# Hybrid decoder trunk on one core: both groups of heads through the attention together, and the norm's broadcast two units later

## The chip, the cores and the metric

The kernel runs on one core of a Trainium2 chip. The metric is the device time of one execution in microseconds. Before the change it was 2619.73 us, the median of three runs (2618.04 to 2623.62). The core has five engines that work side by side from queues of their own: TensorE (PE in the profile; its weight loads are PEld), VectorE (DVE), ScalarE (ACT), GpSimd (POOL) and SyncE (SP), which here issues most DMAs.

## What is computed

Two layers of a decoder trunk run over 576 tokens: 512 of a prompt and 8 x 8 of samples, which share all weights. Each layer is a half-step SwiGLU, a mixer with three branches (causal convolution, gMLP, attention), and another half-step SwiGLU. The change lies in the mixer, in its attention and in the layer norm of its gMLP branch:

```python
def sink_attention(q, k, v, mask, sinks):            # 8 q heads, 2 kv heads, head_dim 64
    s = jnp.einsum('...qkgd,...skd->...kgqs', q, k).astype(jnp.float32) * (HEAD_DIM ** -0.5)
    s = jnp.where(mask, s, NEG_INF)
    sk = sinks.astype(jnp.float32).reshape(N_KV_HEADS, Q_PER_KV, 1)
    m = jnp.maximum(jnp.max(s, axis=-1), sk)
    p = jnp.exp(s - m[..., None])
    denom = jnp.sum(p, axis=-1) + jnp.exp(sk - m)
    p = (p / denom[..., None]).astype(v.dtype)
    return jnp.einsum('...kgqs,...skd->...qkgd', p, v)
...
    g_in = jax.nn.gelu(g_in)
    u = g_in[..., :D_GMLP]
    vg = layer_norm(g_in[..., D_GMLP:], ln_gmlp_g, ln_gmlp_b)
    sg = jnp.einsum('gts,bcsgd->bctgd', w_s, vc) + b_spatial[:, :n].T[None, None, :, :, None]
    y_b = (u * sg.reshape(B, L, D_GMLP)) @ w_gmlp_out
```

The prompt's attention is banded: each chunk of 128 queries sees its own 128 keys and the 128 before. The samples see a cache of 128 keys each and the new tokens.

## The kernel before

Everything lies with features on the partitions and the 576 tokens along the free axis. The projections are exact fp32 products made of three fp32r passes (`mm3`, lines 319 to 329): high x high, high x low, low x high, each on two halves of 288 tokens. One weight tile of four K-tiles gives 24 such matmuls; this is called a unit. After each unit `ftile_parts` calls `steps()` (line 340), which moves every generator in `chains` on by one `yield`. So a side computation is written as a generator, and `wait(n)` in it means: n units of projections before what follows.

Two generators run beside the projections of the mixer. `attention()` (line 765) is one, `sgu()` (line 1008) the other. They issue their matmuls through `cpe`, which gives them a high priority and puts them behind the latest projection matmul; their VectorE and ScalarE work goes through `ave` and `ase` at a lower priority than that of the projections (`ve`, `se`), and the convolution's taps go through `lve` at the lowest. A planner then fixes the order of each engine's queue from these priorities and from its own estimate of when inputs are there; on the chip each queue runs in that order. In this helper all such instructions have line 86 or 88 in the profile, so the reader goes by the names of tiles.

In the attention, both groups of heads lie on partitions: q and k of kv head 0 on rows 0 to 63, those of kv head 1 on rows 64 to 127 (`q4` holds four query heads of each group, `kk` the keys). The values are transposed into `vT`, where a group takes 64 columns. After the rotation of q and k, `sample_scores` and `sample_values` do the samples, and then `scores(c, kv)` and `values` do the prompt, chunk by chunk and, within a chunk, first kv head 0 and then 1. `scores` issues four matmuls of 64 rows into two PSUM tiles of the tag `n` (two buffers in all), adds the mask (VectorE) and calls `soft`, the softmax with the sinks on VectorE and ScalarE. `values` transposes the probabilities, copies them to `ptp` and multiplies them by `vT`: 64 columns of output for the group, which ScalarE copies into `q4`. The list `ready` holds the generators of `values` that are under way; from the scores of a (chunk, group) to its transposes pass five units, and from these to its values two. An iteration is three units, so the eight take 24.

`layer_norm` (line 719) gets its waits as a tuple: W_G = (4, 4, 3, 3) for the gMLP branch. The third is handed to `rstd_steps` (line 387), whose matmuls against `ones` sum the squares, whose Newton steps on VectorE (`newton`, tiles nv, nt, no) make the reciprocal root, and whose matmuls against `idr` broadcast it, split in a high part (ScalarE, line 368) and a low part (VectorE, line 369) in the tile `oh`. The third number is the units between the Newton steps and that broadcast. Behind it follow the normalised rows (tile gv) and `spatial(j)`, four times. `drain(sgu_)` (line 1059) and `drain(att)` (line 1074) run out what is left of either generator.

The rotation of q and k, which comes before the sample scores, swaps halves by DMAs on SP's queue (tile rt), multiplies on GpSimd and VectorE and ends in a copy of the samples' q (tile qs).

Of the kernel before, what the change touches and what calls it, by code (L numbers as in the profile page):

```python
# [12 lines left out]
AF = mybir.ActivationFunctionType  # L13
ALU = mybir.AluOpType
PSUM = bass.MemoryType.PSUM

P = 128
# [19 lines left out]


W_V, W_S, W_N, W_T, W_R, W_B = 2, (2, 1, 1, 1, 1), 3, 2, 6, 1
W_M, W_A = 2, 1  # L40
W_G, W_C = (4, 4, 3, 3), (2, 3, 2)
CHUNKS = ((0, 6), (6, 12), (12, 17), (17, KF))

N_PLAIN = 3
# [15 lines left out]
V_SP = V_CB + 22  # L60
# [35 lines left out]
def trunk(ctx: ExitStack, tc: tile.TileContext, a):  # L96
# [7 lines left out]
    cpe = _At(tc, nc.tensor, HI, mark)  # L104
    ave, ase, age, asy = (_At(tc, e, LOW // 2) for e in (nc.vector, nc.scalar, nc.gpsimd, nc.sync))
# [4 lines left out]
    sp = ctx.enter_context(tc.tile_pool(name="sp", bufs=1))  # L110
# [12 lines left out]
    def big(tag, name, dt=F32, n=1024):  # L123
        return sp.tile([P, n], dt, tag=tag, name=name, bufs=2)
# [8 lines left out]
    def mtile(tag="m"):  # L133
        return zp.tile([P, 512], F32, tag=tag, name=tag)
# [16 lines left out]
    ident = idr.bitcast(F32)  # L151
# [3 lines left out]
    def vcol(l, c, n=1):  # L155
        return vec[:, l, c:c + n]
# [62 lines left out]
    raws, ready = {}, {}  # L219
# [114 lines left out]
    def drain(g):  # L334
        for _ in g:
            pass
        if g in chains:
            chains.remove(g)
# [376 lines left out]
    def wait(n):  # L715
        for _ in range(n):
            yield
# [28 lines left out]
    def mixer(l, xd, nxt):  # L746
# [10 lines left out]
        kk = slot("k", "kk")  # L757
# [7 lines left out]
        def attention():  # L765
# [55 lines left out]
            def soft(s4, sink, view, w, tag):  # L821

                m = tp.tile([P, 4], F32, tag=tag + "m", name="m")
                ave.tensor_reduce(out=m, in_=s4, axis=mybir.AxisListType.X, op=ALU.max)
                ave.tensor_tensor(out=view(m), in0=view(m), in1=sink, op=ALU.max)
                ave.tensor_scalar(out=m, in0=m, scalar1=-1.0, scalar2=None, op0=ALU.mult)
                e = tp.tile([P, 4], F32, tag=tag + "e", name="e")
                ave.tensor_tensor(out=view(e), in0=view(m), in1=sink, op=ALU.add)
                ase.activation(out=e, in_=e, func=AF.Exp)
                d = tp.tile([P, 4], F32, tag=tag + "d", name="d")  # L830
                for j in range(4):
                    ase.activation(out=s4[:, j, :], in_=s4[:, j, :], func=AF.Exp, bias=m[:, j:j + 1], accum_out=d[:, j:j + 1])
                ave.tensor_tensor(out=d, in0=d, in1=e, op=ALU.add)
                ave.reciprocal(out=d, in_=d)
                for j in range(4):
                    ase.activation(out=s4[:, j, :], in_=s4[:, j, :], func=AF.Copy, scale=d[:, j:j + 1])
# [7 lines left out]
            s = big("sp", "ss")[:, 0:768]  # L844
            s4 = s.rearrange("p (k n) -> p k n", k=4)

            def sample_scores():
                for kv in range(2):
                    zz = mtile("n")
                    r = slice(64 * kv, 64 * kv + 64)  # L850
                    for g in range(2):
                        for b in range(4):
                            cpe.matmul(out=zz[32 * b:32 * b + 32, 192 * g:192 * g + P],
                                       lhsT=qs[r, 4 * g + b].rearrange("p j t -> p (j t)"),
                                       rhs=ck[r, P * (4 * g + b):P * (4 * g + b + 1)], start=True, stop=True)
                        cpe.matmul(out=zz[:, 192 * g + P:192 * (g + 1)],
                                   lhsT=qs[r, 4 * g:4 * g + 4].rearrange("p b j t -> p (b j t)"),
                                   rhs=kk[r, TP:T], start=True, stop=True)
                    ave.scalar_tensor_tensor(out=s[:, 384 * kv:384 * (kv + 1)], in0=zz[:, 0:384], scalar=0.125,
                                             in1=con[:, C_MS:C_MS + 384], op0=ALU.mult, op1=ALU.add)  # L860
                sk = vcol(l, V_SS, 2).rearrange("p (k o) -> p k o", o=1).to_broadcast([P, 2, 2])
                soft(s4, sk, lambda t: t.rearrange("p (k g) -> p k g", k=2), 192, "x")

            def sample_values():
                pt = big("pt", "pts")
                zt = mtile("n")
                for i in range(4):
                    cpe.transpose(zt[:, P * i:P * (i + 1)], s4[:, i, 0:P], ident)
                ase.activation(out=pt[:, 0:512], in_=zt, func=AF.Copy)
                zt = mtile("n")  # L870
                for i in range(4):
                    cpe.transpose(zt[0:TS, P * i:P * (i + 1)], s4[:, i, P:192], ident)
                ase.activation(out=pt[0:TS, 512:1024], in_=zt[0:TS, :], func=AF.Copy)
                yield
                zo = mtile("n")
                for kv in range(2):
                    r = slice(64 * kv, 64 * kv + 64)
                    for g in range(2):
                        i = 2 * kv + g
                        cpe.matmul(out=zo[r, P * g:P * (g + 1)], lhsT=vT[0:TS, 4, r], rhs=pt[0:TS, 512 + P * i:512 + P * (i + 1)],  # L880
                                   start=True, stop=False, skip_group_check=True)
                        for b in range(4):
                            bb = 4 * g + b
                            cpe.matmul(out=zo[r, 32 * bb:32 * bb + 32], lhsT=cv[:, P * bb + 64 * kv:P * bb + 64 * kv + 64],
                                       rhs=pt[:, P * i + 32 * b:P * i + 32 * b + 32], start=False, stop=True, skip_group_check=True)
                ave.tensor_copy(out=q4[:, :, TP:T].rearrange("p j (b t) -> p b j t", b=NB),
                                in_=zo[:, 0:256].rearrange("p (b j t) -> p b j t", b=NB, j=4))


            def scores(c, kv):  # L890
                o0 = P if c == 0 else 0
                w = 256 - o0
                k0 = max(c - 1, 0) * P
                r = slice(64 * kv, 64 * kv + 64)
                s4 = big("sp", "sp").rearrange("p (j n) -> p j n", j=4)[:, :, 0:w]
                msk = con[:, C_MP + o0:C_MP + 256].rearrange("p (o n) -> p o n", o=1).to_broadcast([P, 2, w])
                for j in (0, 2):
                    z = mtile("n").rearrange("p (i n) -> p i n", i=2)
                    for i in range(2):
                        cpe.matmul(out=z[:, i, 0:w], lhsT=q4[r, j + i, c * P:(c + 1) * P], rhs=kk[r, k0:k0 + w], start=True, stop=True)  # L900
                    ave.scalar_tensor_tensor(out=s4[:, j:j + 2, :], in0=z[:, :, 0:w], scalar=0.125, in1=msk, op0=ALU.mult, op1=ALU.add)
                soft(s4, vcol(l, V_SP + 4 * kv, 4), lambda t: t, w, "p")
                return values(c, kv, s4, w // P, k0, r)

            def values(c, kv, s4, nk, k0, r):
                pt = big("pt", "ptp")
                for b in range(nk):
                    zt = mtile("n")
                    for j in range(4):
                        cpe.transpose(zt[:, j * P:(j + 1) * P], s4[:, j, b * P:(b + 1) * P], ident)  # L910
                    ase.activation(out=pt[:, 512 * b:512 * (b + 1)], in_=zt, func=AF.Copy)
                yield
                zo = mtile("n")
                for b in range(nk):
                    cpe.matmul(out=zo[r, :], lhsT=vT[:, k0 // P + b, r], rhs=pt[:, 512 * b:512 * (b + 1)],
                               start=(b == 0), stop=(b == nk - 1))
                ase.activation(out=q4[r, :, c * P:(c + 1) * P], in_=zo[r, :].rearrange("p (j n) -> p j n", j=4), func=AF.Copy)


            sample_scores()  # L920
            yield
            ready = [sample_values()]
            for c in range(4):
                for kv in range(2):
                    ready.append(scores(c, kv))
                    yield from wait(W_A)
                    if len(ready) > 2:
                        drain(ready.pop(0))
                    yield
                    next(ready[-2])  # L930
                    yield from wait(W_B)
            drain(ready.pop(0))
            yield
            next(ready[0])
            yield from wait(W_B)
            drain(ready[0])

        att = attention()
        next(att)
# [330 lines left out]
```

## Time and profile before

| | |
|---|---|
| median of three runs | 2619.73 us |
| the profiled execution | 2623.66 us |
| its span, first to last instruction | 2621.9 us |
| TensorE busy | 2584.4 us (99%) |
| VectorE busy | 1909.9 us (73%) |
| ScalarE busy | 1273.5 us (49%) |
| mean granted TensorE clock | 0.995 |

The busy time of TensorE is the union of its matmuls' spans, whose ends are modelled; starts are measured. So what a block of matmuls costs the stream is best read from the start of its first to the start of the next matmul that is not of the block. A form like 64*128 64x256 means 64 rows and 128 columns of the array, and 64 partitions x 256 elements that stream through it. Every fp32 matmul leaves two records, each fp32r matmul one.

### The profile page before, as it was taken

The numbers are of one execution on the slowest core, as the hardware profiler recorded it, in microseconds if no ns is written. First come the engines' busy times: TensorE is split into PE (matmuls) and PEld (weight loads), VectorE is DVE, ScalarE is ACT, GpSimd is POOL, SyncE is SP. The second block draws the span as 40 slices with busy tenths as digits, with TensorE's granted clock in tenths as the row PEclk, the third lists the DMA queues.
The fourth block names the chain that finished last, engine by engine and source line by source line (L and its number), as shares of the span: only waits on it lengthen the run. The fifth ranks groups of instructions, "written<-read, shape, count | busy, mean of one in ns | idle before, by whom it ended". The sixth has DMA issues, their size and how long they took to land.

```text
span 2621.9 us, 49387 instructions
## 1 busy us (share of the span) xinstructions
PE 2584.4 (99%) x18996; PEld 2519.7 (96%) x18996; DVE 1909.9 (73%) x3488; ACT 1273.5 (49%) x2415; POOL 286.9 (11%) x317
## 2 busy tenths in 40 slices
PE   8999999999999999999999999999999999999999
PEld 8999999988899999999999999998989999999999
DVE  8676665688897786766885766747988977756665
ACT  6455453335424564554674554532453245644543
POOL 0111010010010021111110111101100100111110
PEclk9999999999999999999999999999999999999999
DMA  6565454231222464655564655533212234655553
GB/s 178 129 147 130 123 121 129 84 88 58 67 83 81 131 151 124 147 124 131 132 136 119 149 125 132 141 103 85 78 57 73 85 104 123 142 126 137 126 135 95
DMA packets 193920, 303.30 MB, mean 116 GB/s; under 512 B 39434, under 2 KB 56714, under 8 KB 193684
## 3 DMA queue, kind: packets, MB, share of 16 engines
q1 hardware_dynamic: 156820, 233.28, 29.5%
q0 software_dynamic: 36720, 66.86, 15.2%
q8 instruction: 149, 2.44, 0.4%
q14 instruction: 87, 0.71, 0.1%
q10 hardware_dynamic: 144, 0.00, 0.0%
HBM read 221.43 MB, written 8.84 MB: 88 GB/s over the span
## 4 chain that ended last, share of the span: by engine, by line
PE 91%; DVE 3%; DMA 3%; issue 1%; ACT 1%; SPq 0%; POOL 0%; DVEq 0%; POOLq 0%; ACTq 0%
PE z L322 18%; PE z L325 17%; PE z L328 17%; PE z L569 14%; PE n L569 9%; PE m L569 9%; PE n L86 4%; PE m L86 2%; DMA wc<-w_gu 2%; DMA w<-wc 1%; DVE w L88 1%; ACT w L88 1%; DVE u L88 0%; DVE sums L88 0%; DVE x L88 0%
## 5 line engine op out<-in xcount | busy, mean ns | idle before, releaser
L88 ACT ACTIVATE w<-wr 128x512 fp32r<-128x512 f32 (+1 forms) x533 | 324.0, 622 | 657.9 <-PE z L328 526.2
L569 PE MATMUL z<-xh,w 128*128 128x288 f32 x2040 | 443.4, 299 | 5.5 <-DVE z L88 3.7
L88 ACT ACTIVATE w<-wc 128x512 fp32r<-128x512 f32 (+2 forms) x509 | 271.5, 565 | 243.3 <-PE z L328 89.1
L88 DVE TENSOR_TENSOR w<-sums,w 128x512 fp32r<-128x512 f32 x340 | 234.1, 689 | 198.5 <-ACT w L88 194.7
L569 PEld LDWEIGHTS z<-xh,w 128*128 128x128 f32 x2040 | 337.5, 188 | 11.8 <-DVE z L88 5.8
L322 PE MATMUL z<-xh,w 128*128 128x288 f32 x1520 | 337.4, 303 | 8.0 <-ACT w L88 6.6
L88 DVE TENSOR_TENSOR w<-wr,w 128x512 fp32r<-128x512 f32 (+2 forms) x373 | 254.3, 682 | 122.0 <-ACT w L88 121.5
L325 PE MATMUL z<-xl,w 128*128 128x288 f32 x1520 | 328.0, 297 | 0.0
L328 PE MATMUL z<-xh,w 128*128 128x288 f32 x1520 | 327.7, 296 | 0.0
L322 PE MATMUL z<-ah,w 128*128 128x288 f32 x1408 | 303.6, 296 | 0.4
L325 PE MATMUL z<-al,w 128*128 128x288 f32 x1408 | 302.1, 296 | 0.6 <-DVE al L88 0.5
L328 PE MATMUL z<-ah,w 128*128 128x288 f32 x1408 | 301.3, 296 | 0.0
L569 PE MATMUL z<-xl,w 128*128 128x288 f32 x1020 | 300.5, 295 | 0.0
L88 ACT ACTIVATE w<-sums 128x512 fp32r<-128x512 f32 x340 | 212.1, 624 | 176.3 <-PE z L569 90.4
L322 PEld LDWEIGHTS z<-xh,w 128*128 128x128 f32 x1520 | 245.6, 191 | 22.1 <-issue 11.7
L325 PEld LDWEIGHTS z<-xl,w 128*128 128x128 f32 x1520 | 248.2, 191 | 0.7 <-issue 0.7
L328 PEld LDWEIGHTS z<-xh,w 128*128 128x128 f32 x1520 | 246.7, 190 | 0.5 <-issue 0.3
L88 DVE SCALAR_TENSOR_TENSOR c<-cb,vec,c 128x512 f32<-128x512 f32 x480 | 244.5, 556 | 0.2
L322 PEld LDWEIGHTS z<-ah,w 128*128 128x128 f32 x1408 | 226.7, 189 | 2.6 <-DVE x L88 2.3
L325 PEld LDWEIGHTS z<-al,w 128*128 128x128 f32 x1408 | 226.6, 189 | 1.8 <-DVE al L88 1.8
L328 PEld LDWEIGHTS z<-ah,w 128*128 128x128 f32 x1408 | 226.6, 189 | 0.0
L88 POOL DMA_DIRECT2D w<-wc x175 | 150.5, 860 | 616.6 <-ACT w L88 221.3
(255 smaller groups left out, 4854.5 us busy)
## 6 DMA issues: line engine op xcount, KB each, us to landing
wc<-w_gu SPq DMA_DIRECT2D x212, 256.0 KB, 2.9
wr<-w_in SPq DMA_DIRECT2D x184, 256.0 KB, 2.8
w<-wc POOLq DMA_DIRECT2D x175, 256.0 KB, 3.7
wr<-w_gu SPq DMA_DIRECT2D x140, 256.0 KB, 2.8
wr<-w_dn SPq DMA_DIRECT2D x92, 256.0 KB, 2.8
w<-wr POOLq DMA_DIRECT2D x80, 256.0 KB, 4.1
wc<-w_dn SPq DMA_DIRECT2D x36, 256.0 KB, 3.0
wr<-w_out SPq DMA_DIRECT2D x32, 256.0 KB, 3.2
```

Of the source, the lines that this page charges most:

```text
L86: r = f(*args, **kw)
L88: r = f(*args, **kw)
L322: pe.matmul(out=z[c], lhsT=wh, rhs=rh[:, s], start=first, stop=False)
L325: pe.matmul(out=z[c], lhsT=wh, rhs=rl[:, s], start=False, stop=False)
L328: e = pe.matmul(out=z[c], lhsT=wl, rhs=rh[:, s], start=False, stop=last)
L569: e = pe.matmul(out=out, lhsT=w[:, k, :], rhs=r, start=first and k == 0 and i == 0, stop=k == n - 1 and i == 2, skip_group_check=True)
```

## The change

The order of work changes in three places.

In the samples' part, the score matmuls of the two groups are issued in turns, first all those against the cache, then those against the new keys, into two PSUM tiles at once. The value matmuls are issued in turns as well.

In the prompt's part, `scores(c)` and `values(c, ...)` handle both groups of a chunk. The score matmuls of the groups alternate, so that neighbours use rows 0 to 63 and rows 64 to 127 and write different PSUM tiles; the value matmuls alternate between the two halves of the columns of one PSUM tile, and one copy over 128 partitions takes the place of two over 64. The list `ready` is gone: W_A goes from 1 to 4, so four units pass between the scores of a chunk and its transposes, and the values of a chunk come right ahead of the transposes of the next. A chunk takes five units, the whole prompt 20.

In W_G the third number goes from 3 to 5.

```diff
-W_M, W_A = 2, 1
-W_G, W_C = (4, 4, 3, 3), (2, 3, 2)
+W_M, W_A = 2, 4
+W_G, W_C = (4, 4, 5, 3), (2, 3, 2)
...
             def sample_scores():
-                for kv in range(2):
-                    zz = mtile("n")
-                    r = slice(64 * kv, 64 * kv + 64)
-                    for g in range(2):
-                        for b in range(4):
-                            cpe.matmul(out=zz[32 * b:32 * b + 32, 192 * g:192 * g + P],
+                zz = [mtile("n") for kv in range(2)]
+                for g in range(2):
+                    for b in range(4):
+                        for kv, r in enumerate(KV):
+                            cpe.matmul(out=zz[kv][32 * b:32 * b + 32, 192 * g:192 * g + P],
                                        lhsT=qs[r, 4 * g + b].rearrange("p j t -> p (j t)"),
                                        rhs=ck[r, P * (4 * g + b):P * (4 * g + b + 1)], start=True, stop=True)
...
-            def scores(c, kv):
+            def scores(c):
...
-                s4 = big("sp", "sp").rearrange("p (j n) -> p j n", j=4)[:, :, 0:w]
+                s4 = [big("sp", "sp").rearrange("p (j n) -> p j n", j=4)[:, :, 0:w] for kv in range(2)]
...
                 for j in (0, 2):
-                    z = mtile("n").rearrange("p (i n) -> p i n", i=2)
+                    z = [mtile("n").rearrange("p (i n) -> p i n", i=2) for kv in range(2)]
                     for i in range(2):
-                        cpe.matmul(out=z[:, i, 0:w], lhsT=q4[r, j + i, c * P:(c + 1) * P], rhs=kk[r, k0:k0 + w], start=True, stop=True)
-                    ave.scalar_tensor_tensor(out=s4[:, j:j + 2, :], in0=z[:, :, 0:w], scalar=0.125, in1=msk, op0=ALU.mult, op1=ALU.add)
-                soft(s4, vcol(l, V_SP + 4 * kv, 4), lambda t: t, w, "p")
-                return values(c, kv, s4, w // P, k0, r)
+                        for kv, r in enumerate(KV):
+                            cpe.matmul(out=z[kv][:, i, 0:w], lhsT=q4[r, j + i, c * P:(c + 1) * P], rhs=kk[r, k0:k0 + w],
+                                       start=True, stop=True)
+                    for kv in range(2):
+                        ave.scalar_tensor_tensor(out=s4[kv][:, j:j + 2, :], in0=z[kv][:, :, 0:w], scalar=0.125, in1=msk,
+                                                 op0=ALU.mult, op1=ALU.add)
+                for kv in range(2):
+                    soft(s4[kv], vcol(l, V_SP + 4 * kv, 4), lambda t: t, w, "p")
+                return values(c, s4, w // P, k0)
...
                 for b in range(nk):
-                    cpe.matmul(out=zo[r, :], lhsT=vT[:, k0 // P + b, r], rhs=pt[:, 512 * b:512 * (b + 1)],
-                               start=(b == 0), stop=(b == nk - 1))
-                ase.activation(out=q4[r, :, c * P:(c + 1) * P], in_=zo[r, :].rearrange("p (j n) -> p j n", j=4), func=AF.Copy)
+                    for kv, r in enumerate(KV):
+                        cpe.matmul(out=zo[r, :], lhsT=vT[:, k0 // P + b, r], rhs=pt[kv][:, 512 * b:512 * (b + 1)],
+                                   start=(b == 0), stop=(b == nk - 1), skip_group_check=True)
+                ase.activation(out=q4[:, :, c * P:(c + 1) * P], in_=zo.rearrange("p (j n) -> p j n", j=4), func=AF.Copy)
...
             sample_scores()
-            yield
-            ready = [sample_values()]
+            yield from wait(W_A)
+            last = sample_values()
+            next(last)
+            yield from wait(W_B)
             for c in range(4):
-                for kv in range(2):
-                    ready.append(scores(c, kv))
-                    yield from wait(W_A)
-                    if len(ready) > 2:
-                        drain(ready.pop(0))
-                    yield
-                    next(ready[-2])
-                    yield from wait(W_B)
-            drain(ready.pop(0))
-            yield
-            next(ready[0])
-            yield from wait(W_B)
-            drain(ready[0])
+                g = scores(c)
+                yield from wait(W_A)
+                drain(last)
+                last = g
+                next(last)
+                yield from wait(W_B)
+            drain(last)
```

## Rows read from the trace of the kernel before

**Rows 1.** The page: busy time by engine (part 1), the chain (part 4).
```profile
PE 2584.4 (99%) x18996; PEld 2519.7 (96%) x18996; DVE 1909.9 (73%) x3488; ACT 1273.5 (49%) x2415; POOL 286.9 (11%) x317
...
PE 91%; DVE 3%; DMA 3%; issue 1%; ACT 1%; SPq 0%; POOL 0%; DVEq 0%; POOLq 0%; ACTq 0%
```

**Rows 2.** TensorE by line and shape: count | busy us, mean ns | idle before.
```profile
L86 PE MATMUL n<-ptp,vT 128*64 128x512 f32 x56 | 27.5, 607 | 0.0
L86 PE MATMUL n<-kk,q 64*128 64x256 f32 x96 | 24.4, 391 | 0.0
...
L86 PE MATMUL n<-kk,q 64*128 64x128 f32 x32 | 4.6, 285 | 0.0
```

**Rows 3.** Timeline of TensorE, waits: start us, us, operation xcount [idle before <-releaser].
```profile
339.58 2.41 PE L569 MATMUL n<-f,w 128*128 128x288 f32 x12 [1.74 <-DVE u L88]
...
535.65 0.82 PE L86 MATMUL m<-idr,oh 128*128 128x128 f32 x2 [3.32 <-ACT oh L368]
...
1829.99 0.55 PE L86 MATMUL m<-idr,oh 128*128 128x128 f32 x2 [2.53 <-ACT oh L368]
...
1831.91 1.80 PE L86 MATMUL m<-idr,oh 128*128 128x128 f32 x8 [0.77 <-DVE oh L369]
...
1868.91 1.11 PE L86 MATMUL n<-idr,ss 128*128 128x128 f32 x6 [0.34 <-ACT ss L88]
```

**Rows 4.** Timeline of TensorE: a score block and the split one, each with its follower.
```profile
596.60 1.99 PE L86 MATMUL n<-kk,q 64*128 64x256 f32 x8
598.52 0.53 PE L322 MATMUL z<-xh,w 128*128 128x288 f32 x2
...
657.45 1.13 PE L86 MATMUL n<-kk,q 64*128 64x256 f32 x4
658.51 0.53 PE L322 MATMUL z<-xh,w 128*128 128x288 f32 x2
```

**Rows 5.** Timeline of TensorE: a values block and its follower.
```profile
648.16 1.93 PE L86 MATMUL n<-ptp,vT 128*64 128x512 f32 x4
650.03 0.53 PE L322 MATMUL z<-xh,w 128*128 128x288 f32 x2
```

**Rows 6.** Timeline of TensorE: the start of the sample scores.
```profile
558.30 0.42 PE L86 MATMUL n<-ck,qs 64*32 64x128 f32 x8
558.66 0.43 PE L86 MATMUL n<-kk,qs 64*128 64x64 f32 x2
559.02 0.42 PE L86 MATMUL n<-ck,qs 64*32 64x128 f32 x8
```

**Rows 7.** Timeline of TensorE: the sample values, the start of two sets.
```profile
584.83 0.43 PE L86 MATMUL n<-pts,vT 64*64 64x128 f32 x2
...
585.77 0.43 PE L86 MATMUL n<-pts,vT 64*64 64x128 f32 x2
```

**Rows 8.** Windows: length, busy us (xcount) by engine, granted clock, DMA share, GB/s.
```profile
535.60:545.40 9.80, 9.67 (x37) 8.96 (x38) 7.50 (x13) 3.40 (x7) 2.27 (x4) 0.50 0.30 87
1830.00:1839.10 9.10, 8.33 (x36) 7.80 (x37) 7.10 (x12) 2.99 (x6) 2.56 (x3) 0.62 0.32 94
340.00:345.00 5.00, 5.00 (x28) 5.00 (x28) 5.00 (x11) 1.60 (x3) 0.18 (x1) 0.66 0.76 168
```

**Rows 9.** Timeline of VectorE: the low part of the factor; the samples' q.
```profile
537.36 0.15 DVE L369 TENSOR_TENSOR oh<-no,oh 128x5 fp32r<-128x5 f32 x1
...
555.77 0.28 DVE L88 COPY qs<-q 128x256 f32<-128x256 f32 x1
```

**Rows 10.** Windows again, PE, PEld, DVE, ACT, POOL in this order.
```profile
533.30:555.80 22.50, 20.07 (x116) 19.36 (x117) 20.18 (x30) 8.74 (x16) 9.24 (x8) 0.77 0.36 86
558.30:600.00 41.70, 41.66 (x336) 37.90 (x336) 39.75 (x97) 20.20 (x60) 4.87 (x6) 1.00 0.24 72
```

**Rows 11.** Timelines of VectorE and ScalarE: a softmax's first and last steps.
```profile
629.80 1.29 DVE L88 SCALAR_TENSOR_TENSOR sp<-n,con 128x512 f32<-128x512 f32 x2
...
637.12 1.70 ACT L88 ACTIVATE sp<-sp,d 128x256 f32<-128x256 f32 x4
```

## What I expect of the change

> **What bounds the kernel now.** I read the page first: TensorE is busy for 99% of the span and the chain that ended last lies on it for 91% [rows 1]. So a microsecond taken out of its stream counts, as long as nobody else becomes late. The stretch that the change touches is the mixer of each layer. Its time splits into the full-width projection matmuls (two of 0.132 us each per merged entry of the timeline) and the attention's small fp32 blocks that are pushed in between. The groups by line show the two large kinds: 96 records of scores and 56 of values [rows 2]; every fp32 matmul leaves two records. The reader should see in the timeline what one such block costs the stream, and that TensorE never idles among them. The one place in this stage where it does idle is the normalisation of the gMLP branch, at 535 us and again at 1830 us [rows 3].
>
> **Scores of the prompt.** A block of 8 records holds TensorE from 596.60 to 598.52, 1.92 us; a block of 4 holds it from 657.45 to 658.51, 1.06 us [rows 4]. So a record costs 0.215 us and entering and leaving the half-height form about 0.20 us a block. Per layer and for blocks 1 to 3 there are six blocks of 8. After, each chunk has two blocks (heads 0 and 1, then 2 and 3), because the four score tiles share two PSUM buffers and the second pair waits for VectorE; each again has 8 records, but 4 of each group of heads, in rows 0 to 63 and 64 to 127. If the two halves of the array run side by side, such a block takes the time of 4 records: 6 x 1.92 = 11.5 us becomes 6 x 1.06 = 6.4, and 5.2 us go (one of the six is already split, which adds 0.2). If they don't, nothing is saved. Chunk 0 has narrower blocks: 4.6 us for the four in both layers [rows 2], 1.15 each; by the same halving 0.9 us a layer.
>
> **Values of the prompt.** Four records take from 648.16 to 650.03, 1.87 us [rows 5], two about 1.0. Both groups now fill the two column halves of one block: three blocks of 1.87 and one of 1.0 fall away a layer, 6.6 us. Merging also halves the evacuations into q4 on ScalarE, which cost nothing either way, since ScalarE is busy for 49% [rows 1].
>
> **Sample part.** The four sets of scores follow each other every 0.72 us (558.30 to 559.02) [rows 6]; issued in pairs, half of 2.87 us goes, 1.4. The four sets of values take 0.94 us each (584.83 to 585.77) [rows 7]; half of 3.76 is 1.9.
>
> **Do packed matmuls overlap in fp32?** For column groups the trace says yes: eight records of the cache scores, four column groups, take 0.42 us and hold the next one off by 0.36, the same as two records alone (0.43 and 0.36) [rows 6]. For row groups no row of before shows it; the bounds are nothing and one half, and I take one half, by the nearest row, the column groups. Sum for a layer 5.2 + 0.9 + 6.6 + 1.4 + 1.9 = 16.0 us, 32 us for both. The Trainium skill (TensorE: Matmul & The Clock Gate, Part 3) gives 3.07x for four row tiles and 2.38x for three column tiles, not 4 and 3; an estimate from its 77%, 1.54x for two, would make the 32 us about 22. The row of four column groups shows no such loss.
>
> **The norm's broadcast.** The program reaches it at 532.33 and idles 3.32 us until ScalarE's half of the factor is there; in layer 1 it idles 2.53 and 0.77 us [rows 3]. The idle time also costs the clock: the granted clock is 0.50 over the next 9.8 us and 0.62 over 9.1 us in layer 1 [rows 8], so 4.9 and 3.5 us more. Together 3.3 + 4.9 = 8.2 and 3.3 + 3.5 = 6.8, 15.0 us. Two units are 48 projection matmuls, 6.3 us, so TensorE would arrive at 538.6 and 1833.8; the later half of the factor ends at 537.5 [rows 9] and was in use at 1831.91 [rows 3]. So this stall goes whole.
>
> **What is late next.** The sample scores need the copy of q, which ends at 556.05, only 2.25 us before they start at 558.30 [rows 6, 9]. That slack existed because TensorE had lost 8.2 us. Behind it stand the rotations of q on VectorE, with their DMAs on SP's queue and the multiply on GpSimd. From 533.3 to 555.8 VectorE is busy for 20.2 of 22.5 us [rows 10], so with all its idle time gone and the two vt operations (0.87 us) moved behind, the copy comes 3.2 us earlier. TensorE would then wait 8.2 - 2.25 - 3.2 = 2.8 us in layer 0; for layer 1, with the same slack, 1.3. The bounds are 0 (the convolution's taps, the lowest priority, fall behind the copy) and these; I take 4.1, because VectorE is the busier of the two there. A wait of 1.74 us at 339.58 was followed by a clock of 0.66 over 5 us [rows 3, 8], 1.7 us lost; I add it once. The norm's part is 15.0 - 4.1 - 1.7 = 9.2 us.
>
> **The other moved waits.** Scores to transposes were five units for one group; now they are four units for two. One group's softmax takes from 629.80 to 638.82 [rows 11], 9.0 us between other work, and two overlap on VectorE and ScalarE; four units are 12.7 us plus the small blocks inside, about 16. That is tight. The one place where a softmax was just late idled TensorE 0.34 us [rows 3]. For eight chunks I take 0.3 us each, 2.4, with bounds 0 and 0.8 each; behind a waiting transpose stand all projection matmuls. The gMLP steps after the broadcast also come two units later, which leaves the last of them (15 small matmuls) to be issued together where the generator is drained, without units between them and their transposes. At worst they wait for one copy and one subtraction, some 1.5 us a layer; I take nothing, since the product that uses them comes three projections later and the score block that is split in two shows that projections are put between blocks that wait [rows 4].
>
> **Sum.** 32.0 + 9.2 - 2.4 = 38.8 us. The profiled execution took 2623.66 us (span 2621.9 and 1.8 around it), 3.9 above the median of the runs shown; the gain has nothing to do with that difference, so 2623.66 - 38.8 = 2584.9 for it, and 2619.73 - 38.8 = 2581 against the median.
>
> **The rivals.**
> - Row halves don't overlap, column halves do. Speaks for it: no row shows two row groups at once. Lost: 5.2 + 0.9 and about 0.9 of the sample scores, 7.0 a layer: 2595 us.
> - Both overlap, but each pass gets slower while a second stream reads its operand. A pair of score passes then takes between 0.215 us (no loss) and 0.43 (no gain); at 0.28, three tenths of the way, 16.0 a layer shrinks by 4.8: 2591 us. Against it: the eight-record row [rows 6]. This is what the 77% of the Trainium skill (same page and part) would do here.
> - The change does not do what it says: no overlap at all. Left are the fewer entries of merged blocks (about 2 us a layer) and the norm: 2609 us.
> - The stall moves whole to the sample scores: idle as computed, and the clock falls as long as it did before, 4.9 + 3.5 instead of 1.7: 2588 us.
> - VectorE becomes the bound. From 558.3 to 600 it is busy 39.75 of 41.7 us [rows 10], while I take about 7 us of TensorE's time out of that stretch; if 5 of these come back in each layer, 2591 us.
> - Slower: the two softmaxes don't fit in four units and TensorE waits at the transposes of all eight chunks, long enough to lose the clock as in layer 1's stall, 6.8 us each: 54 in place of the 2.4, 2633 us. It decides from about 5.2 us a chunk (41.2 / 8). For it: 16 us against a chain of 9 that is run twice; against it: the projections that are put in between.
>
> **How the numbers follow.** Chances: forecast 0.50 (its own range 2567 to 2592), row halves 0.11, slower passes 0.08, no overlap 0.05, moved stall 0.14, VectorE 0.04, two late softmaxes 0.08. The shortest time is full overlap, no new wait and no softmax wait: 32 + 15, 2572 us; with 0.2 us a block on either side of the fixed costs 2567. The range goes up to the rival of the row halves with some of the waits' upper bound, 2600. Left out are no overlap, late softmaxes and a little. A measurement of this kernel can tell 0.2%, 5.2 us. All cases but the last lie further below; of its 0.08, 0.02 fall within (waits of 36 to 46 us in all). So faster 0.92, same 0.02, slower 0.06.
>
> **What would show it.** Right: score blocks of 8 records that take 1.06 us and values blocks of 8 records that take 1.9; starts of the two row groups within a few hundredths of a microsecond; no idle time before the broadcast and the clock at 1.00 after it. Wrong: score blocks of 1.9 us, idle time before the first sample scores above 3 us or before the transposes above 1 us, or a granted clock below 1.00 between 545 and 700 us.

## The result and the profile after

The changed kernel takes 2605.51 us, the median of four runs (2603.23 to 2608.89), against 2620.32 for the kernel before (2618.04 to 2623.62), run beside it. The ratio is 0.9944 with a 95% interval of 0.9926 to 0.9961: 14.8 us faster, where 38.8 were forecast. Its profiled execution took 2605.83 us, with a span of 2604.1.

The page of the changed kernel, busy time by engine and the chain:

```profile
PE 2553.3 (98%) x18996; PEld 2501.7 (96%) x18996; DVE 1910.1 (73%) x3488; ACT 1265.6 (49%) x2407; POOL 290.2 (11%) x317
...
PE 86%; DVE 7%; DMA 3%; issue 2%; ACT 1%; POOL 0%; SPq 0%; DVEq 0%; POOLq 0%; ACTq 0%
```

TensorE's busy time fell by 31.1 us (2584.4 to 2553.3, [rows 1]), the span by only 17.8. The difference is idle time that was not there before, and the chain shows on whom TensorE waits: VectorE's share of it went from 3% to 7%. In the traces the two mixers got shorter by 10.1 and 9.4 us; what lies outside them differs by 1.7 the other way. What the packing did is plain in TensorE's groups by shape (count | busy us, mean ns of one | idle before):

```profile
L86 PE MATMUL n<-kk,q 64*128 64x256 f32 x96 | 17.8, 403 | 1.7 <-DVE sp L88 1.7
...
L86 PE MATMUL n<-ptp,vT 128*64 128x512 f32 x56 | 13.8, 607 | 0.0
...
L86 PE MATMUL n<-kk,q 64*128 64x128 f32 x32 | 4.5, 340 | 5.2 <-DVE sp L88 4.3 <-ACT pts L88 0.9
```

The values went from 27.5 to 13.8 us, exactly half [rows 2], and the sample groups (pts and qs) from 15.5 to 7.9. The scores of chunks 1 to 3 went from 24.4 only to 17.8, and those of chunk 0 from 4.6 to 4.5. The timeline of TensorE shows why (start us, us, operation, idle before):

```profile
602.05 1.13 PE L86 MATMUL n<-kk,q 64*128 64x256 f32 x8
603.12 0.74 PE L86 MATMUL m<-ws,vt 128*128 128x256 f32 x4
604.17 1.73 PE L86 MATMUL n<-kk,q 64*128 64x256 f32 x8 [0.32 <-DVE sp L88]
605.83 0.39 PE L86 MATMUL m<-ws,vt 128*128 128x256 f32 x1
...
630.00 1.13 PE L86 MATMUL n<-kk,q 64*128 64x256 f32 x8
631.06 0.54 PE L322 MATMUL z<-xh,w 128*128 128x288 f32 x2
...
646.40 1.94 PE L86 MATMUL n<-ptp,vT 128*64 128x512 f32 x8
648.27 0.44 PE L86 MATMUL n<-idr,sp 128*128 128x128 f32 x2
```

In chunks 1 and 2 the first block holds TensorE for 1.06 us (630.00 to 631.06); that and 1.87 for a values block are as forecast. The second block, heads 2 and 3, holds it for 1.66 (604.17 to 605.83) and begins with a wait: the two groups get their PSUM buffers back one VectorE operation after the other, so not all of the block runs side by side. In chunk 3 both blocks take about 1.5 us (653.61 to 655.16, 657.08 to 658.57).

The new waits of layer 0, in the same timeline, the broadcast first:

```profile
535.48 1.34 PE L86 MATMUL m<-idr,oh 128*128 128x128 f32 x10
...
549.27 1.11 PE L86 MATMUL n<-ck,qs 64*32 64x128 f32 x32 [2.74 <-DVE qs L88]
...
566.48 0.52 PE L86 MATMUL m<-ws,vt 64*128 64x128 f32 x3 [1.33 <-DVE sg L1007]
...
576.26 0.71 PE L86 MATMUL n<-kk,q 64*128 64x128 f32 x6 [0.87 <-ACT pts L88]
...
580.87 1.04 PE L86 MATMUL n<-kk,q 64*128 64x128 f32 x8 [2.25 <-DVE sp L88]
```

The 3.32 us ahead of the broadcast are gone [rows 3]. In their place come 2.74 us ahead of the sample scores and, up to 581, three more waits. With smaller ones behind them layer 0 now idles 8.4 us and layer 1 8.5, where it was 3.3 and 3.6. The granted clock falls with them. Windows of the changed kernel (length, busy us of PE, PEld, DVE, ACT, POOL, then the granted clock):

```profile
546.00:552.00 6.00, 3.26 (x48) 2.52 (x47) 6.00 (x10) 4.33 (x7) 2.33 (x4) 0.76 0.72 197
552.00:556.00 4.00, 4.00 (x19) 3.96 (x18) 4.00 (x8) 0.00 (x0) 1.85 (x2) 0.51 0.21 65
1852.00:1857.00 5.00, 4.62 (x23) 4.58 (x24) 4.83 (x14) 2.43 (x6) 0.80 (x1) 0.66 0.16 56
1867.00:1872.00 5.00, 5.00 (x24) 4.78 (x25) 2.61 (x9) 0.23 (x1) 0.00 (x0) 0.50 0.17 52
```

Read the third busy time of the first two lines: VectorE works for all of 546 to 556 us. The two kernels compare best over the stretch in which they do the same 1584 projection matmuls, from shortly before the broadcast to some 5 us before the end of the convolution's last taps. First the kernel before, then the changed one:

```profile
526.62:801.47 274.85, 271.42 (x1914) 250.67 (x1913) 247.49 (x499) 116.34 (x261) 29.61 (x23) 0.98 0.25 75
```

```profile
523.72:788.50 264.78, 256.40 (x1915) 242.37 (x1914) 247.32 (x499) 112.25 (x257) 30.72 (x23) 0.99 0.26 78
```

Both do the same 499 VectorE instructions in 247.4 us. In the kernel before VectorE idled 27.4 us there (274.85 - 247.49); the change took 10.1 us out of the stretch, and VectorE now idles 17.5. The forecast wanted 19.4 a layer, which would have left 8. That is the thread of the experiments.

### The profile page after: what moved, and what is told of

Same layout as the page of the kernel before. It is cut to its first block, busy times and chain, and to the rows that moved or that the text cites. A ratio compares the mean times of both kernels' runs of the same rounds, so it can differ in the third digit from the quotient of the medians.

```text
span 2604.1 us, 49406 instructions
## 1 busy us (share of the span) xinstructions
PE 2553.3 (98%) x18996; PEld 2501.7 (96%) x18996; DVE 1910.1 (73%) x3488; ACT 1265.6 (49%) x2407; POOL 290.2 (11%) x317
## 3 DMA queue, kind: packets, MB, share of 16 engines
q0 software_dynamic: 36720, 66.86, 15.4%
## 4 chain that ended last, share of the span: by engine, by line
PE 86%; DVE 7%; DMA 3%; issue 2%; ACT 1%; POOL 0%; SPq 0%; DVEq 0%; POOLq 0%; ACTq 0%
PE z L322 17%; PE z L325 17%; PE z L328 16%; PE z L569 14%; PE n L569 9%; PE m L569 9%; PE n L86 2%; DVE c L88 2%; DMA wc<-w_gu 2%; DVE w L88 1%; PE m L86 1%; DMA w<-wc 1%; ACT w L88 1%; DVE u L88 1%; DVE sums L88 0%
## 5 line engine op out<-in xcount | busy, mean ns | idle before, releaser
L88 DVE SCALAR_TENSOR_TENSOR c<-cb,vec,c 128x512 f32<-128x512 f32 x480 | 250.1, 570 | 0.1
```

What stands on the lines that cost most here:

```text
L88: r = f(*args, **kw)
```

## The experiments

**Theory A:** VectorE sets the pace of the mixer once TensorE is faster. Its queue has a fixed order, with the convolution's taps put in between, so what TensorE saves is waited out again. **Rival B:** the new waits come from the attention's own chains (two groups in four units) and from the second block of the scores. **Rival C:** packing is worth little.

**The norm alone.** The kernel before with one number changed:

```diff
-W_G, W_C = (4, 4, 3, 3), (2, 3, 2)
+W_G, W_C = (4, 4, 5, 3), (2, 3, 2)
```

> The kernel before with the third number of W_G at 5, nothing else. The traces of before and after put some 16.6 us of the gain on the stretch of the norm, net of the 2.7 and 1.2 us that TensorE then waits for the copy of q. Theory A (VectorE has no room left from 545 to 590 us once the old stall is gone, so what is saved there is waited out again): 8 to 13 us faster than before, with TensorE idle ahead of the first sample scores by 2 to 3 us and again between 560 and 585 us. Rival B (the new waits come from the attention's own chains of two groups in too few units): 15 to 17 us faster, and no idle time after the sample scores. Rival C (the attention's new order costs, not the norm): the same time as B.

It took 2621.31 us, ratio 0.9996 (0.9986 to 1.0007): no gain that the runs can tell, less than any theory expected. The timeline of TensorE and the window behind it:

```profile
552.39 0.65 PE L86 MATMUL n<-ck,qs 64*32 64x128 f32 x8 [2.83 <-DVE qs L88]
```

```profile
552.39:562.00 9.61, 9.61 (x61) 7.57 (x62) 9.05 (x17) 2.89 (x6) 3.72 (x5) 0.50 0.32 103
```

The stall at the broadcast went, and 2.83 us of it came back ahead of the sample scores, with a clock of 0.50 over the next 9.61 us, 4.8 us lost. That is 7.6 of the 8.2 us that the old stall had cost. No idle time follows between 560 and 585 us, which theory A had expected here. In this one traced execution the stretch of the 1584 projections is 273.56 us, 1.3 shorter than before, and that of layer 1 270.60, 4.8 shorter (before 275.42); the rest of the span is 3.7 longer, and no run explains that.

**The attention alone.** The changed kernel with the old number:

```diff
-W_G, W_C = (4, 4, 5, 3), (2, 3, 2)
+W_G, W_C = (4, 4, 3, 3), (2, 3, 2)
```

> The changed kernel with the third number of W_G back at 3, so the old 3.3-us stall and its slow clock remain and only the attention is packed. Theory A (VectorE load; the stall lets VectorE catch up): 18 to 30 us faster than before, that is much more than the 3 us that the attention's stretch gave in the changed kernel, and TensorE idle under 1 us in all between 560 and 590 us. Rival B (the chains of two groups in four units are too long by themselves): 2 to 8 us faster, with the same waits at the score blocks of chunk 0 (2.2 us) as in the changed kernel.

2606.96 us, ratio 0.9934 (0.9921 to 0.9946): 15.4 us faster than before, all that the whole change gives, and between what A and B expected. So the two parts don't add: 1 and 15 make 15. The timeline of TensorE shows that theory A's idle time "under 1 us" was wrong as well:

```profile
531.68 0.55 PE L86 MATMUL m<-idr,oh 128*128 128x128 f32 x2 [2.70 <-ACT oh L368]
...
583.05 1.06 PE L86 MATMUL n<-kk,q 64*128 64x128 f32 x8 [3.76 <-DVE sp L88]
```

The old stall doesn't let VectorE catch up for good; TensorE waits for it anyway 50 us later. By this the packing alone already uses the slack up.

**Group after group.** The changed kernel with the loops over the groups outermost again, in the same blocks:

```diff
-                    for i in range(2):
-                        for kv, r in enumerate(KV):
+                    for kv, r in enumerate(KV):
+                        for i in range(2):
```

(and so for the sample scores and values and the prompt's values)

> The changed kernel with its score and value matmuls issued group after group within the same blocks, in the same units, so that row halves and column halves have no neighbour to run beside. If packing saves 16 us a layer on TensorE and the waits eat it only between 545 and 590 us (theory A), the blocks after 590 us (scores of chunks 1 to 3, values) lose their 11 us a layer and those before lose little: 18 to 28 us slower than the changed kernel, so slower than before by 4 to 13. If packing saves nothing that counts: within 5 us of the changed kernel.

2611.66 us, ratio 0.9953 (0.9941 to 0.9966): 10.7 us below the kernel before that ran beside it, against 14.8 for the changed kernel. So it lost 4 us and not 18 or more. But this run didn't undo what it was meant to undo, as the timeline of TensorE shows:

```profile
633.16 1.14 PE L86 MATMUL n<-kk,q 64*128 64x256 f32 x8
634.23 0.54 PE L322 MATMUL z<-xh,w 128*128 128x288 f32 x2
```

The block takes 1.07 us, as with the turns. Two matmuls of one group followed by two of the other still run side by side. So do the sample scores against the cache, with eight of a group in a row: 32 records in 0.64 us, with the turns 0.60 (1835.14 to 1835.74):

```profile
1840.13 0.70 PE L86 MATMUL n<-ck,qs 64*32 64x128 f32 x32 [2.27 <-DVE qs L88]
1840.77 1.12 PE L86 MATMUL n<-kk,qs 64*128 64x64 f32 x8
```

Only the sample values lost it, where ten matmuls of a group come in a row, in two shapes by turns (pts with vT, then with cv): their main group (pts, cv) is busy for 5.2 us again, against 2.6. The run falls within 5 us of the changed kernel once each is set against its own neighbour, which was the sign of rival C, yet it says nothing on it, since little packing was undone; the halved values in the profile after do speak against it.

**Without the taps.** The changed kernel and the kernel before, each with the first of the 31 taps only; a third and a fourth with one of the two parts:

```diff
-            for k in range(CW):
+            for k in range(1):
```

> The changed kernel with only the first of the convolution's 31 taps; the other 30 are left out, which takes work from VectorE alone. Theory A: the waits between 545 and 590 us shrink to under 1.5 us a layer in all and the kernel gains most of the 24 us by which the forecast was missed: 2575 to 2590 us. Rival B (latency of the chains, not VectorE's load): the waits stay, 2600 to 2606 us.

> The kernel before with only the first of the convolution's 31 taps (the other 30 are left out), the partner of the changed kernel with one tap, which took 2589.9 us. Theory A (the forecast's gain is there as long as VectorE's queue isn't full of taps between 533 and 600 us): 2618 to 2623 us, since in the kernel before TensorE waits for VectorE hardly anywhere; so the change would be worth 28 to 33 us without the taps against 15 with them. Rival B (the taps cost both kernels the same): about 2605 us, a difference of 15 us as with the taps.

> The kernel before with the third number of W_G at 5 and with the first of the convolution's 31 taps only (30 are left out). Without taps the kernel before took 2629.5 us, waiting 6.3 and 7.6 us for the copy of q, and the changed one 2589.9. Theory A (VectorE's load made the norm's gain vanish): the gain of the norm comes back, 2605 to 2612 us, and the wait for the copy of q is under 1 us. Rival (the norm's two units only move a stall, whatever VectorE does): 2620 us or more with an idle time ahead of the sample scores above 3 us.

> The changed kernel with the third number of W_G back at 3 and with one tap of 31 (30 left out): the attention's packing alone, without VectorE's load. By the forecast's own terms the packing is worth 32 - 2.4 us, so 2600 us beside the 2629.5 of the kernel before with one tap; and the time is 10 us or more above the changed kernel with one tap (2589.9). If the packing is worth only what it gave with the taps, 15 us: 2614 us.

Each against the kernel before, with all its taps, that ran beside it (2620.3 to 2622.9 us):

| | all taps, us | one tap, us |
|---|---|---|
| kernel before | 0 | +6.6 (2629.48) |
| norm alone | -1.1 | -10.6 (2610.79) |
| attention alone | -15.4 | -22.4 (2599.01) |
| both | -14.8 | -32.4 (2589.94) |

With VectorE relieved, and counted from the kernel before with one tap, the attention is worth 29.0 us (22.4 + 6.6; forecast 29.6), the norm on top of it 10.0 (forecast 9.2), both 39.0 (forecast 38.8). With all taps the same instructions on TensorE give 15.4, nothing (14.8 against 15.4) and 14.8. The chains of the attention are the same in both columns, so the taps take the larger part of what is missing, as theory A says. The agreement with the forecast is better than it deserves, though. In the other order, the norm first, the norm is worth 17.2 us (10.6 + 6.6) and the attention 21.8 (32.4 - 10.6; with all taps 13.7), so the taps cost the attention between 8 and 14 us, and the two parts don't add without taps either. The kernel before with one tap came out at 2629.5 us, above what was expected of it; in the timeline of TensorE of this kernel and then of the changed one with one tap:

```profile
556.49 0.65 PE L86 MATMUL n<-ck,qs 64*32 64x128 f32 x8 [6.31 <-DVE qs L88]
```

```profile
549.16 0.67 PE L86 MATMUL n<-ck,qs 64*32 64x128 f32 x32
```

Without the taps the norm's factor is early, and the whole stall sits ahead of the sample scores. There VectorE idles 4.49 us for a DMA, by the order of the program that of the last rotation, which SP issued only at 547.4, behind DMAs of the gMLP. Two units more for the norm put those DMAs behind the rotations, and the wait is gone (with the attention alone and one tap it is there, 5.05 us). So the norm's 10.0 us are the end of another stall than the one that was forecast, and that they match 9.2 is luck; part of the 39.0 is a longer stall of the kernel before, and counted from the one with all taps it is 32.4. The attention alone lies 9.1 us above both together, where 10 or more were expected.

Rival B keeps a share too. The changed kernel with one tap was expected to wait under 1.5 us a layer between 545 and 590 us. It waits 0.90 there in layer 0, but 2.66 in the same part of layer 1, and over the whole mixers 2.7 and 4.4, where the norm alone with one tap waits 0.9 in each. The longest wait is that of a product of the gMLP that comes after ScalarE's part of the samples' softmax:

```profile
1843.37 0.52 PE L86 MATMUL m<-ws,vt 64*128 64x128 f32 x3 [2.44 <-ACT ss L88]
```

**The taps later.** All work is kept, but fewer taps are put into VectorE's queue before 592 us and more behind it:

```diff
-F_GLU, F_B, F_U, F_BY, F_CG, F_CY, F_A = 3, 3, 3, 2, 3, 3, 4
+F_GLU, F_B, F_U, F_BY, F_CG, F_CY, F_A = 2, 2, 4, 3, 3, 3, 4
```

and, in the second run, 1, 1, 4, 4 for the first four.

> The changed kernel with all its work, but the fillers that put the convolution's taps into VectorE's queue set to 2, 2, 4, 3 in place of 3, 3, 3, 2 per projection (GLU, gates, u, outputs of gMLP): 12 taps of about 1.05 us a layer leave the stretch before 592 us and go behind it, where VectorE idles 12 us up to 690. Theory A: the waits between 545 and 590 us (8 us a layer in the changed kernel) shrink by half or more, 8 to 16 us faster than the changed kernel, 2590 to 2598 us. Rival B (the attention's own chains): within 3 us of the changed kernel, 2603 to 2609.

> The same with 1, 1, 4, 4: 18 to 22 taps a layer moved behind 592 us, about twice as much as VectorE has idle time there up to 690. Theory A: the waits before 590 us go almost wholly, but new ones come behind 600 us or at the convolution's norm; 2588 to 2598 us. Rival B: as the changed kernel or slower, 2603 to 2612.

2606.48 us (ratio 0.9935, 0.9917 to 0.9953) and 2615.94 (0.9972, 0.9961 to 0.9983): not to be told from the changed kernel (0.9944), and slower than it. Theory A's figures failed in both, and the first run came out where rival B had put it (2603 to 2609). The second shows that it need not be for B's cause. Up to 690 us it had no wait for q and gained 20 us in layer 0, twice as much as the changed kernel. Then, in windows and the timeline of TensorE:

```profile
710.00:790.00 80.00, 74.94 (x558) 73.70 (x558) 80.00 (x150) 19.28 (x31) 12.68 (x7) 1.00 0.24 76
804.00:812.00 8.00, 5.59 (x28) 5.03 (x29) 5.51 (x13) 2.04 (x4) 0.00 (x0) 0.79 0.17 57
```

```profile
806.41 1.33 PE L86 MATMUL m<-lns,ones 128*128 128x288 f32 x2 [2.96 <-DVE lns L723]
```

From 710 to 790 us VectorE is busy for all 80 us and TensorE waits for 5 of them; at 806 the convolution's norm waits for the last taps, and the clock falls. So the taps aren't misplaced by carelessness. They have to be done by about 800 us, and VectorE is full from 700 on in both kernels (79.57 of 80 us in the changed one from 710 to 790). What is put off early is missing late.

**Less time for the same taps.** From 700 to 800 us GpSimd does eight additions a layer of 1.8 us. In the changed kernel, VectorE's taps (ns: shortest/median/longest) and one such addition:

```profile
L88 DVE SCALAR_TENSOR_TENSOR c<-cb,vec,c x100: 269/739/1453, 709.9 to 789.3; 128x512 f32<-128x512 f32 x50, 128x64 f32<-128x64 f32 x50
```

```profile
721.78 1.81 POOL L88 TENSOR_TENSOR M<-M,gt 128x576 f32<-128x576 f32 x1 [7.76 <-DVE gt L88]
```

A tap of 64 columns, 0.28 us as a rule, took 1.45 when it started during the addition, until that was done. The Trainium skill (Advanced Engine Details and Errata, Miscellaneous Facts, GPSIMD Details) says that GpSimd shares a read and a write interface with VectorE and conflicts with VectorE instructions that have two inputs in SBUF, as a tap has; the trace agrees, with 1.2 us for the tap above. So the taps stay later and the additions go to VectorE, at 0.75 us each:

```diff
-            add_branch(i, gate("t", "gt", F_CG), (ch, cl), ge)
+            add_branch(i, gate("t", "gt", F_CG), (ch, cl), ve)
```

> The changed kernel with the fillers 2, 2, 4, 3 (as in the run with the taps later, which gained 14.7 us in layer 0 up to 690 us against 10.2 of the changed kernel, and gave 2.4 back where the convolution ends), and with the 8 additions of the attention branch on VectorE in place of GpSimd, whose 1.8-us operations hold up one tap each by 1.2 us from 700 to 800 us. Theory A (the end of VectorE's queue of taps sets the end): 8 x 1.2 us of waiting go and 8 x 0.75 us of work come, 3.4 us a layer, so the 2.4 us stay gained: 2596 to 2602 us. Rival (the end of the taps doesn't count): 2603 to 2608 us as with the taps later alone.

2597.64 us, ratio 0.9905 (0.9892 to 0.9919), as theory A expected and clear of the changed kernel's interval. The additions on VectorE without the later taps were not run. The longest tap of that stretch is now 0.76 us:

```profile
L88 DVE SCALAR_TENSOR_TENSOR c<-cb,vec,c x108: 275/516/758, 709.3 to 788.0; 128x512 f32<-128x512 f32 x54, 128x64 f32<-128x64 f32 x54
```

**Four PSUM buffers for the scores.** The second block of a chunk writes to the buffers of tag m, so it needn't wait for those of the first:

```diff
-                    z = [mtile("n").rearrange("p (i n) -> p i n", i=2) for kv in range(2)]
+                    z = [mtile("n" if j == 0 else "m").rearrange("p (i n) -> p i n", i=2) for kv in range(2)]
```

> The changed kernel with the scores of heads 2 and 3 of each chunk written to the two PSUM buffers of tag m, which the gMLP uses, in place of those of tag n that VectorE has still to read. If the second block of a chunk is dear (1.6 to 2.3 us against 1.16 for the first) because its two groups get their buffers one VectorE operation after the other, all four pairs of a chunk now run in one block or two of 1.06 us: 0.5 to 1.2 us for each of six blocks and about 2 for the two of chunk 0, 4 to 8 us in both layers, 2597 to 2602 us. If the second block is dear for another reason, or if the gMLP's products then wait for their buffers: 2605 us or more.

> The same as the last one with the scores of heads 2 and 3 in the PSUM buffers of tag m as well, which by itself took the changed kernel to 2601.9 us. If both gains are of different waits: 2592 to 2598 us, faster than either kernel. If VectorE's total work up to the convolution's norm is the bound, it ends no earlier than the last one: 2596 to 2602 us.

Alone it took 2601.89 us (0.9920, 0.9902 to 0.9937), 21.0 below the kernel before beside it where the changed kernel is 14.8 below, with intervals that overlap. Together with the later taps and the additions on VectorE it took 2590.65 (2590.11 to 2593.56), 7.0 below the run without it (2593.97 to 2599.55), beside which it ran, and a little below what was expected. The ratio to the kernel before is 0.9882 (0.9869 to 0.9896): 30.8 us, twice the gain of the change. A chunk's 16 records now take 1.93 us (624.69 to 626.62) in its timeline of TensorE, and its stretch of the same 1584 projections is 258.52 us, here behind that of the run without the four buffers:

```profile
624.69 1.14 PE L86 MATMUL n<-kk,q 64*128 64x256 f32 x8
625.66 1.03 PE L86 MATMUL m<-kk,q 64*128 64x256 f32 x8
626.62 0.53 PE L322 MATMUL z<-xh,w 128*128 128x288 f32 x2
```

```profile
526.21:787.13 260.92, 255.92 (x1914) 241.65 (x1913) 240.13 (x503) 112.24 (x257) 16.50 (x15) 0.99 0.26 79
523.77:782.29 258.52, 253.54 (x1915) 240.44 (x1913) 240.54 (x503) 112.35 (x257) 16.13 (x15) 0.99 0.26 79
```

VectorE's work there fell from 247.3 to 240.5 us, and it idles 18.0, about as in the changed kernel. That the stretch got shorter by about as much as VectorE's work (6.3 against 6.8) is chance: the later taps and the moved additions took 7.2 us of work out, in part to behind the stretch's end, and shortened it by 3.9; the four buffers took another 2.4 at the same work. So VectorE's work bounds the stretch from below, but its length also hangs on where VectorE and TensorE wait for each other. Some 18 us of VectorE's idle time remain, and no run tried to remove them.

## Why the prediction was wrong

The step that failed is the one that let VectorE follow: the forecast took 19.4 us a layer out of a stretch in which VectorE idles 27.4, and charged 6.5 us of idle time and 1.7 of slow clock in all. The runs showed 16.9 and about 8.5 in their place, and with VectorE relieved of 30 taps the changed kernel gains another 17.6 us (32.4 against 14.8). Besides, the second score block was mis-sized. Term by term:

**Row halves and column halves overlap: right.** 1.06 us for a score block, 1.87 for a values block, as worked out [rows 4, 5]. The rivals without overlap, or with slower passes, fell.

**The second score block: mis-sized.** The forecast gave it 1.06 us like the first. It takes 1.66, because the second group's buffer comes free one VectorE operation, about 0.6 us, later (two take 1.29 [rows 11]); with four buffers both blocks together took 1.93. The busy time of both score shapes fell by 6.7 us (29.0 to 22.3) where 12.2 were counted, 5.5 short.

**The norm: the stall went, its gain didn't.** The idle time of 2.8 us ahead of the sample scores in layer 0 was forecast to the tenth (2.83 with the norm alone, 2.74 with both), and 1.3 in layer 1 (0.7 and 1.21). The tenth is luck: with the norm alone, counted from the start of the stretch, TensorE arrives 8.9 us earlier where 8.2 were worked out, and the copy of q ends 3.8 earlier where it was 3.2, so two errors of the same size cancel. What failed here is the clock behind it: 1.7 us, taken from a wait of 1.74 us [rows 3, 8]; measured 4.8 in layer 0 with the norm alone and 3.4 (1.4 + 2.0) in the changed kernel. That was the rival in which the stall moves whole, with a chance of 0.14.

**VectorE: the rival was there, at 0.04 and 5 us a layer.** VectorE had 4.3 us of idle time between 533 and 600 us [rows 10], and the forecast took 15 out of just that stretch, 8.2 of the stall and about 7 of the packing. The forecast noted it and gave no ground for so low a chance; for the copy of q it took 0 as a bound, because the taps have the lowest priority. But a priority only orders a queue when the kernel is built; on the chip the tap ahead is done first, and at 800 us all of them are due.

**The softmax waits: the wrong place.** 2.4 us were put ahead of the transposes, which never wait for a softmax in the changed kernel. TensorE waits a step earlier, where the scores need their buffers: 6.9 us ahead of the score groups (1.7 and 5.2). The gMLP's steps, taken at nothing, wait 1.33 and 0.32 us in layer 0 and 1.43, 2.63 and 0.33 in layer 1, 6.0 in all.

**The sum.** Idle time in both mixers is 16.9 us, against 6.5 that the forecast charged (4.1 + 2.4): 10.4 more. The slow clock costs about 8.5 (1.4, 2.0, 1.7 and 2.5 in the four windows above, 0.9 in two more of layer 1) against 1.7: 6.8 more, and no less than it cost before the change (4.9 + 3.5 [rows 8]). The score blocks fell short by 5.5. Together that is 22.7. All this is read in the two traced executions, which differ by 17.8 us where 38.8 were forecast, so 21.0 are missing there, 19.3 of them in the mixers (24.0 by the medians). The sums overlap by some 3 us, since a window of slow clock holds some idle time and some of the score blocks.

## What to carry to other kernels

Before counting what a faster engine saves, lay the next-busiest engine beside it over the same stretch: its idle time there (27 us a layer here, at 90% busy) is the most that can be saved as long as its work stays the same, and a fixed queue yields only part of it. Two changes that lie in one stretch need not add; measure each alone, and with the busy engine relieved, before trusting a sum. And where one engine's time is short, look for what holds its instructions up as well as for what they do: eight additions a layer moved off GpSimd, with the taps shifted to match, gave 9 us (23.8 against 14.8).

## What the hardware showed unexpectedly

A stall's price here was mostly the clock: 2.83 us of idle time were followed by 9.61 us at 0.50 of full speed, so the level of 1.2 GHz in place of 2.4. Not every wait has that price: behind the 2.25 us ahead of 580.87 in the changed kernel the clock stayed at 1.00, and no run here shows what decides it.

```profile
580.00:584.00 4.00, 3.13 (x24) 3.01 (x25) 3.61 (x11) 0.13 (x1) 0.00 (x0) 1.00 0.20 66
```

Matmuls on different rows need not stand in turns to run side by side: with two of one group and then two of the other the block took 1.07 us, with turns 1.06, and the records start in pairs some 13 ns apart instead of 6 to 7. Eight of a group in a row kept the overlap in the sample scores, and two and two on column halves in the prompt's values (busy 13.8 us either way); ten in a row, in two shapes by turns, lost it in the sample values. Whether the number or the change of shape did that stays open. The Trainium skill (TensorE: Matmul & The Clock Gate, Part 3) says that matmuls start in strict order. By that rule only the middle two of the four could overlap, and an estimate from the block before [rows 4] would be six records of 0.215 and 0.20, 1.5 us; the measurement decides. The records don't name their rows, so which of them started when is inferred: from the time of the block, and from the order of TensorE's queue, in which the groups stand two and two.

VectorE and GpSimd aren't independent: a tap of 0.28 us lasted 1.45 beside an addition on GpSimd, and without such additions no tap of that stretch took more than 0.76 us, the 512 columns included.
